# A triangular solve turned round: column updates instead of row sums, its turned copy taken in pieces, some blocks moved from ScalarE to VectorE, and norm factors broadcast by transposes

## The chip, the cores and the metric

The kernel runs on one core of one Trainium2 chip. The metric is the device time of one execution in microseconds; a kernel's time is the median of its runs. Beside those runs stands one execution that was taken with the hardware profiler, and all rows of the trace are from that one.

## The reference

The reference is a small network over 256 tokens of width 1024: a first block of two layers (four gated feed-forward parts, an RWKV-7 time mix in the first layer, a differential attention in the second) and a second block (sliding-window and stick-breaking attention, then a mixture of 16,384 small experts). The change touches two things in it.

The first is the recurrence of the RWKV-7 time mix, per head, with 16 heads of 64 columns:

```python
def step(S, inp):
    r_t, w_t, k_t, v_t, a_t, b_t = inp
    sa = jnp.einsum('bhij,bhj->bhi', S, a_t)
    S = S * w_t[:, :, None, :] + sa[..., None] * b_t[:, :, None, :] + v_t[..., None] * k_t[:, :, None, :]
    return S, jnp.einsum('bhij,bhj->bhi', S, r_t)
```

The kernel does not step through the 256 tokens. It works in chunks of 128 tokens, where the terms `sa` of one chunk solve a triangular system; for that it inverts the 32x32 unit lower-triangular blocks on the diagonal of each head's and chunk's system.

The second is the factor of each RMS norm, `rsqrt(mean(x*x) + eps)`, which is one number per token (or per token and head) and is multiplied onto rows that lie across partitions.

## The kernel before

Activations lie transposed, with 128 of the 1024 columns on the partitions and the 256 tokens along the free axis. Weights come in tiles of 128x1024 (512 KB) by SyncE's queue into three `raw` buffers. Work is written as Python generators that are advanced in turn (`stagger`, `staggered`, `parallel`); this fixes the program order, and the framework's scheduler then lays down one fixed order of instructions for each engine when the kernel is built, with program order as priority. Each engine takes its instructions strictly in that order.

The part around the change, in the time mix (`rwkv`, `keys`, class `Wkv`):

- `rproj` makes the r and the v projections on TensorE. A v projection of one of the eight `d` (two heads each) is 16 matmul instructions (8 tiles, two instructions each in fp32) into one of two PSUM banks `mm`, which ScalarE copies out into `vf` (L526). While v is projected, `prep` for the first two `d` also runs: four transposes (`tr`, L397), their copy, and for each of four systems the matmuls `gr` and VectorE's masked copy `gm` (L1210).
- `chain` runs beside it (`parallel`, 1.25 steps of it for one of `rproj`): first `key(d)` for each `d`, which among other things normalizes k by `gstat_g` and makes `gram`, whose diagonal 32x32 blocks POOL gathers into `bdg`; then `solve`.
- `solve` holds the 128 diagonal blocks (16 heads by 2 chunks by 4 blocks) as one 32x32 matrix on each of the 128 partitions. It turns `bdg` into `sysb` with a 32x32 block transpose, and then for t = 1 to 31 makes row t of the inverse `xs` out of the rows above it: one VectorE multiply of t*t elements (L656), in which `xs` is read with a stride of 32 elements, and one VectorE sum over t (L658). At the end a block transpose writes `xd`; ScalarE copies `xs` with its last two axes swapped into `xr` (L662); a second block transpose writes `xtd` (L663).
- `Wkv.head(d)` then begins, for each `d`, with 16 small copies: the four 32-token blocks of `xd` into `x1`, then those of `xtd` into `xt1` (L1227, ScalarE, tile `xb`, one instruction for four systems of 32x32, eight instructions for each `d`; there are two such pairs of buffers). The first matmuls `lp` read `xt1`; the matmuls `lx` read `x1`. After that come the chains of small matmuls and copies (`ch`, `rt`, `ut`, `sp`), the mean (`mn`), and the norm by `gstat_g`. Up to five heads' generators are in flight.
- `gstat_g` makes a norm's factors: matmuls `smp` with a mask, VectorE's scale (L333), POOL's power -0.5 (L336), for two groups a copy into `re` (L340), and then two fp32 matmuls of 128x128 against the identity, which lay the factors out across the free axis (L345).

Of the kernel before, what the change touches and what calls it, by code (L numbers as in the profile page):

```python
# [6 lines left out]
F32 = mybir.dt.float32  # L7
F32R = mybir.dt.float32r
U32 = mybir.dt.uint32
AF = mybir.ActivationFunctionType  # L10
ALU = mybir.AluOpType
AX = mybir.AxisListType
# [127 lines left out]
def staggered(gens, every, width=99):  # L140
    queue, active, t = list(gens), [], 0
    while queue or active:
        if queue and len(active) < width and (t >= every or not active):
            active.append(queue.pop(0))
            t = 0
        t += 1
        for g in list(active):
            try:
                next(g)
            except StopIteration:  # L150
                active.remove(g)
        yield


def parallel(a, b, ratio):
    debt, live = 0.0, [True, True]
    while any(live):
        if live[0]:
            live[0] = next(a, live) is not live
        debt += ratio if live[0] else 1  # L160
        while live[1] and debt >= 1:
            live[1] = next(b, live) is not live
            debt -= 1
# [10 lines left out]
class Net:  # L174
# [150 lines left out]
    def gstat_g(self, sq, mask, G, scale, eps, op=ALU.add, sb=None):  # L325
        nc = self.nc
        pb = self.smt()
        ps = pb[:, T:T + 2 * G]
        for h in range(2):
            self.mm(ps[:, h * G:(h + 1) * G], sq[:, h * 128:(h + 1) * 128], mask, h == 0, h == 1)  # L330
        yield
        ms = self.small(4)
        nc.vector.tensor_scalar(ms[:, :2 * G], ps, scale, eps, op0=ALU.mult, op1=op)  # L333
        yield
        r = self.small(4)
        nc.gpsimd.tensor_tensor(r[:, :2 * G], ms[:, :2 * G], self.mhalf[:, :2 * G], op=ALU.pow)  # L336
        yield
        if G > 1:
            re = self.tmp("re")
            nc.vector.tensor_copy(re.rearrange("p (a b) -> p a b", a=2 * G),  # L340
                                  r[:, :2 * G, None].to_broadcast([128, 2 * G, 128 // G]))
            yield
        for h in range(2):
            st = re[:, h * 128:(h + 1) * 128] if G > 1 else r[:, h:h + 1].to_broadcast([128, 128])
            self.mm(pb[:, h * 128:(h + 1) * 128], st, self.ident, h == 0, h == 1)  # L345
        yield
        if sb is None:
            return pb[:, :T]
        nc.scalar.activation(sb, pb[:, :T], AF.Copy)
        return sb  # L350
# [232 lines left out]
    def keys(self, er, rproj, aa, cum, ar, bt, kt, xd, xtd, oka, gram):  # L583
        tc, nc, i = self.tc, self.nc, self.i
        vec = self.v
        D = range(8)
        bdg = er.tile([128, 32, 32], F32, name="bdg", tag="sya")
        sysb = er.tile([128, 32, 32], F32, name="sysb")
        pb = er.tile([128, 2, 16], F32, name="pb")
        xs = er.tile([128, 32, 32], F32, name="xsys")  # L590
        flat = lambda a: a.rearrange("p a b -> p (a b)")
        nc.gpsimd.memset(xs, 0.0)
        nc.gpsimd.memset(flat(xs)[:, 0:1024:33], 1.0)
        cmid = cum[:, :, :, 64:65].rearrange("p a b o -> p (a b o)")
        nc.vector.tensor_scalar(pb[:, 0], cmid, E05, None, op0=ALU.mult)
        nc.vector.tensor_scalar(pb[:, 1], cmid, -E05, None, op0=ALU.mult)
        dcy = self.dcy
        v1 = lambda a: a.rearrange("p (c t) -> p c t", c=2)

        ready = set()  # L600

        def key(d):
            kr = kt[:, d].rearrange("p c t -> p (c t)")
            sq = self.tmp("sq")
            nc.scalar.activation(sq, kr, AF.Square, scale=vec("k_k", d))
            yield
            en = self.tmp("en")
            dc = self.small(2)
            nc.scalar.activation(dc[:, 0:1], cum[:, d, 0, 128:129], AF.Exp, scale=-E05, bias=pb[:, 0, 2 * d:2 * d + 1])
            nc.scalar.activation(dc[:, 1:2], cum[:, d, 1, 64:65], AF.Exp, scale=-E05)  # L610
            for c in range(2):
                j = 2 * d + c
                nc.scalar.activation(en[:, c * 128:(c + 1) * 128], cum[:, d, c, 1:], AF.Exp, scale=E05, bias=pb[:, 1, j:j + 1])
                nc.scalar.activation(cum[:, d, c], cum[:, d, c], AF.Exp, scale=-E05, bias=pb[:, 0, j:j + 1])
            ready.add(d)
            rb = yield from self.gstat_g(sq, self.bmask2, 2, 1.0, 1e-24, op=ALU.max)
            nc.vector.tensor_tensor(dcy[:, d:d + 1], dc[:, 0:1], dc[:, 1:2], op=ALU.mult)
            kn = self.tmp("kn")
            nc.vector.scalar_tensor_tensor(kn, kr, vec("k_k", d), rb, op0=ALU.mult, op1=ALU.mult)
            ep = cum[:, d]  # L620
            nc.vector.scalar_tensor_tensor(ar[:, d, :, 0], v1(kn), -1.0, ep[:, :, :128], op0=ALU.mult, op1=ALU.mult)
            t = self.tmp("ka")
            nc.vector.tensor_tensor(t, kn, aa[:, d], op=ALU.mult)
            nc.vector.tensor_tensor(bt[:, d], v1(t), v1(en), op=ALU.mult)
            yield
            ps = []
            for hh in range(2):
                hs = slice(64 * hh, 64 * hh + 64)
                p = self.wkt("bd")
                for c in range(2):  # L630
                    self.mm(p[:, c * 128:(c + 1) * 128], bt[hs, d, c], ar[hs, d, c, 0], c == 0, c == 1)
                ps.append(p)
            t = self.tmp("kb")
            nc.vector.tensor_scalar(t, aa[:, d], vec("k_a", d), oka[:, d:d + 1], op0=ALU.mult, op1=ALU.add)
            nc.vector.tensor_tensor(t, t, kr, op=ALU.mult)
            nc.vector.tensor_tensor(kt[:, d], v1(t), v1(en), op=ALU.mult)
            yield
            for hh in range(2):
                nc.scalar.activation(gram[:, d, 2 * hh:2 * hh + 2], ps[hh][:, :T].rearrange("p (c t) -> p c t", c=2), AF.Copy)
            yield  # L640
            for b in range(4):
                bs = slice(32 * b, 32 * b + 32)
                nc.gpsimd.tensor_copy(bdg[bs, :, 4 * d:4 * d + 4].rearrange("p t h -> p h t"), gram[bs, d, :, bs])
            yield

        def rout(d, p):
            while d not in ready:
                yield
            nc.vector.tensor_tensor(ar[:, d, :, 1], v1(p), cum[:, d, :, 1:], op=ALU.mult)
            yield  # L650

        def solve():
            nc.vector.transpose(flat(sysb), flat(bdg))
            for t in range(1, 32):
                tmp = er.tile([128, 32, 32], F32, name="stmp")
                nc.vector.tensor_tensor(tmp[:, :t, :t], xs[:, :t, :t].rearrange("p j s -> p s j"),  # L656
                                        sysb[:, t, None, :t].to_broadcast([128, t, t]), op=ALU.mult)
                nc.vector.tensor_reduce(xs[:, t, :t], tmp[:, :t, :t], axis=AX.X, op=ALU.add)  # L658
                yield
            nc.vector.transpose(flat(xd), flat(xs))  # L660
            xr = er.tile([128, 32, 32], F32, name="xr", tag="sya")
            nc.scalar.activation(xr, xs.rearrange("p t s -> p s t"), AF.Copy)  # L662
            nc.vector.transpose(flat(xtd), flat(xr))  # L663

        def chain():
            yield from staggered([key(d) for d in D], EVERY["keys"])
            yield from solve()

        parallel(rproj(rout), chain(), EVERY["krat"])
# [485 lines left out]
class Wkv:  # L1155
# [58 lines left out]
    def head(self, d):  # L1214
        net = self.net
        nc, vec = net.nc, net.v
        ar, bt, kt, gg, vf, tab, xd, xtd, gram = self.a
# [3 lines left out]
            yield  # L1221
        pair = self.x1s[d % 2]
        x1, xt1 = pair[:, 0], pair[:, 1]
        for src, dst in ((xd, x1), (xtd, xt1)):
            for b in range(4):
                bs = slice(32 * b, 32 * b + 32)
                nc.scalar.activation(dst[bs, :, bs], src[bs, :, 4 * d:4 * d + 4].rearrange("p t h -> p h t"), AF.Copy)  # L1227
        yield
        while d >= EVERY["nb"] and d - EVERY["nb"] not in self.ended:
            yield  # L1230
# [4 lines left out]
        p = net.wkt("lp")  # L1235
# [6 lines left out]
        p = net.wkt("lx")  # L1242
# [9 lines left out]
        for c in range(2):  # L1252
            bank = net.wkt("ch")
            p, pu, o = (bank[:, 128 * n:128 * n + 128] for n in range(3))
# [45 lines left out]
        p = net.wkt("mn")  # L1300
# [58 lines left out]
```

## Time and profile before

| what | value |
|---|---|
| time, median of 3 runs | 2231.76 us (2227.08 to 2232.41) |
| profiled execution, its own time | 2242.64 us |
| span of the profiled execution | 2240.9 us |
| TensorE matmul busy | 2196.6 us (98%) |
| TensorE weight load busy | 2054.8 us (92%) |
| VectorE busy | 1544.6 us (69%) |
| ScalarE busy | 1121.9 us (50%) |
| GpSimd busy | 77.0 us (3%) |
| mean granted TensorE clock | 0.985 |

The profiled execution took 10.9 us longer than the median run; the span, from its first to its last instruction, is 1.7 us shorter than its own time. Busy times are sums over the span, and a busy TensorE is not one at its peak, since the ends of its matmuls are modelled. The granted clock is a share of full speed: 1.00 is 2.4 GHz and 0.50 is 1.2 GHz.

### The profile page before, as it was taken

Reading aid. Unit: us, or ns where it says so; the run is one execution under the profiler, and the core shown is the slowest. Engines: PE = TensorE matmul, PEld = TensorE weight load, DVE = VectorE, ACT = ScalarE, POOL = GpSimd, SP = SyncE. Lnnn points to the kernel's source line nnn. Section 1 sums busy time; section 2 is a strip of 40 time slices with the busy share of each in tenths; the row PEclk is TensorE's granted clock in tenths of the full one; section 3 lists DMA queues with packets and bytes.
Section 4 is the critical chain, followed back from the end, with each engine's and each line's share of the span. In section 5 each row is a group of like instructions: output and inputs, shape, how many; then the busy total and the mean of one; then the engine's idle time right before and its main releaser. Section 6 shows DMA issues by size and latency. Waiting matters only on the chain.

```text
span 2240.9 us, 40442 instructions
## 1 busy us (share of the span) xinstructions
PE 2196.6 (98%) x16114; PEld 2054.8 (92%) x16114; DVE 1544.6 (69%) x2966; ACT 1121.9 (50%) x2083; POOL 77.0 (3%) x109
## 2 busy tenths in 40 slices
PE   8999999989999999999999999999999999999999
PEld 8998877779999999979999999999999999888887
DVE  6666694666666666476665777899678995666565
ACT  5443723335445444465445664445566664554544
POOL 0000140000000100020000100000000000000000
PEclk9999996999999999999999999999999999999999
DMA  6554321015565455534556345455544445555554
GB/s 212 185 179 135 121 95 38 1 61 192 182 181 182 165 170 176 167 113 160 179 181 194 132 138 184 157 168 178 192 138 139 132 136 185 195 191 197 191 195 150
DMA packets 98588, 351.05 MB, mean 157 GB/s; under 512 B 10944, under 2 KB 12480, under 8 KB 98272
## 3 DMA queue, kind: packets, MB, share of 16 engines
q1 hardware_dynamic: 98400, 348.48, 47.8%
q8 instruction: 126, 2.06, 0.4%
q14 instruction: 62, 0.51, 0.1%
HBM read 347.38 MB, written 1.05 MB: 155 GB/s over the span
## 4 chain that ended last, share of the span: by engine, by line
PE 47%; DVE 5%; issue 1%; ACT 0%; DMA 0%; POOLq 0%; POOL 0%; ACTq 0%
PE mm L243 27%; PE y L243 16%; PE pg L243 3%; DVE wl L258 2%; DVE dm L1125 1%; DVE ex L1130 0%; DVE dm L1128 0%; PE sc L243 0%; PE po L243 0%; DVE v L1093 0%; PE smp L243 0%; PE tr L757 0%; PE psc L243 0%; DVE si L1095 0%; DMA raw<-in_p_u_dram 0%
## 5 line engine op out<-in xcount | busy, mean ns | idle before, releaser
L243 PE MATMUL mm<-xs,wh 128*128 128x256 f32 x6304 | 1159.3, 285 | 13.2 <-ACT wh L255 7.0
L243 PEld LDWEIGHTS mm<-xs,wh 128*128 128x128 f32 x6304 | 986.4, 192 | 20.0 <-ACT wh L255 7.2
L258 DVE TENSOR_TENSOR wl<-raw,wh 128x1024 fp32r<-128x1024 f32 (+1 forms) x633 | 765.3, 1209 | 325.3 <-ACT wh L255 324.1
L255 ACT ACTIVATE wh<-raw 128x1024 fp32r<-128x1024 f32 (+1 forms) x633 | 660.3, 1044 | 594.3 <-PE mm L243 399.5
L243 PE MATMUL mm<-xs,wl 128*128 128x256 f32 x3152 | 894.4, 284 | 2.4 <-DVE wl L258 2.4
L243 PEld LDWEIGHTS mm<-xs,wl 128*128 128x128 f32 x3152 | 605.7, 192 | 3.4 <-DVE wl L258 3.3
L243 PE MATMUL y<-wh,cs 128*128 128x512 f32 x1024 | 273.8, 389 | 0.0
L243 PE MATMUL mm<-hh,wh 128*128 128x256 f32 x1408 | 250.1, 281 | 0.0
L243 PEld LDWEIGHTS y<-wh,cs 128*128 128x128 f32 x1024 | 192.1, 188 | 39.8
L243 PEld LDWEIGHTS mm<-hh,wh 128*128 128x128 f32 x1408 | 215.8, 188 | 0.0
L243 PE MATMUL mm<-hh,wl 128*128 128x256 f32 x704 | 197.8, 281 | 0.0
L243 PE MATMUL y<-wl,cs 128*128 128x512 f32 x512 | 157.5, 389 | 0.0
L243 PEld LDWEIGHTS mm<-hh,wl 128*128 128x128 f32 x704 | 132.5, 188 | 0.0
L243 PE MATMUL mm<-xs,raw 128*128 128x256 f32 x512 | 126.5, 395 | 2.5 <-DVE xs L490 2.5
L243 PEld LDWEIGHTS y<-wl,cs 128*128 128x128 f32 x512 | 96.1, 188 | 20.0
L243 PEld LDWEIGHTS mm<-xs,raw 128*128 128x128 f32 x512 | 96.2, 197 | 17.1 <-DVE xs L490 2.6
L306 ACT ACTIVATE cs<-ga 128x256 fp32r<-128x256 f32 x103 | 43.0, 418 | 136.9 <-PE y L243 136.6
L420 DVE TENSOR_TENSOR gu<-mm,rstd 128x512 f32<-128x512 f32 x88 | 60.8, 691 | 47.0 <-PE mm L243 45.5
L306 ACT ACTIVATE hh<-hv 128x256 fp32r<-128x256 f32 x88 | 36.6, 416 | 104.5 <-DVE hv L425 104.5
L307 DVE TENSOR_TENSOR cs<-ga,cs 128x256 fp32r<-128x256 f32 x103 | 43.7, 425 | 55.1 <-ACT cs L306 55.1
L1040 DVE TENSOR_SCALAR ohb<-iota,xT 128x128 f32<-128x128 f32 x192 | 59.3, 341 | 15.4 <-PE pg L243 13.9
L243 PE MATMUL pg<-ohb,xT 128*128 128x128 f32 x512 | 65.8, 275 | 0.0
(318 smaller groups left out, 1954.0 us busy)
## 6 DMA issues: line engine op xcount, KB each, us to landing
raw<-in_ffn_in_dram SPq DMA_DIRECT2D x176, 512.0 KB, 3.3
raw<-in_p_u_dram SPq DMA_DIRECT2D x128, 512.0 KB, 3.3
raw<-in_p_v_dram SPq DMA_DIRECT2D x128, 512.0 KB, 3.3
raw<-in_ffn_out_dram SPq DMA_DIRECT2D x64, 512.0 KB, 3.6
raw<-in_w_in_dram SPq DMA_DIRECT2D x34, 512.0 KB, 3.3
raw<-in_ffn_out_dram SPq DMA_DIRECT2D x32, 384.0 KB, 3.4
raw<-in_w_rkv_dram SPq DMA_DIRECT2D x24, 512.0 KB, 3.3
raw<-in_w_kv_dram SPq DMA_DIRECT2D x16, 512.0 KB, 3.3
```

What stands on the lines that cost most here:

```text
L243: self.nc.tensor.matmul(out, lhsT, rhs, start=start, stop=stop, skip_group_check=True)
L255: hi = nc.scalar.activation(fh[:rows, :w], raw[:rows, :w], AF.Copy)
L258: lo = nc.vector.tensor_tensor(fl[:rows, :w], raw[:rows, :w], fh[:rows, :w].bitcast(F32), op=ALU.subtract)
L306: nc.scalar.activation(dst[rows, :T], src, AF.Copy)
L307: nc.vector.tensor_tensor(dst[rows, T:], src, dst[rows, :T].bitcast(F32), op=ALU.subtract)
L420: nc.vector.tensor_tensor(t, p.rearrange("p (a b) -> p a b", a=2), box["r"][:, None, :].to_broadcast([128, 2, T]), op=ALU.mult)
L1040: nc.vector.tensor_scalar(b, iota, itp[:, 1, t:t + 1], itp[:, 2, t:t + 1], op0=ALU.is_equal, op1=ALU.mult)
L1125: nc.vector.tensor_tensor(m, iota[:, None, :50].to_broadcast([128, 16, 50]), bf[:, h, :, None].to_broadcast([128, 16, 50]), op=ALU.is_equal)
```

## The change

`solve` goes by columns: at step t, row t of the inverse is final, and its multiples are added to all rows below it. One multiply makes (31-t)*(t+1) products, one add puts them onto those rows; in both the innermost axis has unit stride (or repeats one element). The copy with swapped axes is taken in four pieces, three of them inside the loop, after t = 15, 23 and 28. The block transpose for `xtd` goes ahead of that for `xd`. In `head`, the blocks of `xt1` are copied ahead of those of `x1`, and for d = 0 and 1 VectorE makes the copies instead of ScalarE. In `gstat_g`, the two fp32 matmuls against the identity become two transposes.

```diff
@@ gstat_g
             st = re[:, h * 128:(h + 1) * 128] if G > 1 else r[:, h:h + 1].to_broadcast([128, 128])
-            self.mm(pb[:, h * 128:(h + 1) * 128], st, self.ident, h == 0, h == 1)
+            nc.tensor.transpose(pb[:, h * 128:(h + 1) * 128], st, self.ident)
@@ keys
         def solve():
             nc.vector.transpose(flat(sysb), flat(bdg))
-            for t in range(1, 32):
+            xr = er.tile([128, 32, 32], F32, name="xr", tag="sya")
+            turned = 0
+            for t in range(31):
+                n, w = 31 - t, t + 1
                 tmp = er.tile([128, 32, 32], F32, name="stmp")
-                nc.vector.tensor_tensor(tmp[:, :t, :t], xs[:, :t, :t].rearrange("p j s -> p s j"),
-                                        sysb[:, t, None, :t].to_broadcast([128, t, t]), op=ALU.mult)
-                nc.vector.tensor_reduce(xs[:, t, :t], tmp[:, :t, :t], axis=AX.X, op=ALU.add)
-                yield
+                nc.vector.tensor_tensor(tmp[:, :n, :w], xs[:, t, None, :w].to_broadcast([128, n, w]),
+                                        sysb[:, w:, t, None].to_broadcast([128, n, w]), op=ALU.mult)
+                nc.vector.tensor_tensor(xs[:, w:, :w], xs[:, w:, :w], tmp[:, :n, :w], op=ALU.add)
+                if t in (15, 23, 28):
+                    nc.scalar.activation(xr[:, :, turned:w], xs[:, turned:w].rearrange("p t s -> p s t"), AF.Copy)
+                    turned = w
+                yield
+            nc.scalar.activation(xr[:, :, turned:], xs[:, turned:].rearrange("p t s -> p s t"), AF.Copy)
+            nc.vector.transpose(flat(xtd), flat(xr))
             nc.vector.transpose(flat(xd), flat(xs))
-            xr = er.tile([128, 32, 32], F32, name="xr", tag="sya")
-            nc.scalar.activation(xr, xs.rearrange("p t s -> p s t"), AF.Copy)
-            nc.vector.transpose(flat(xtd), flat(xr))
@@ Wkv.head
-        for src, dst in ((xd, x1), (xtd, xt1)):
+        for src, dst in ((xtd, xt1), (xd, x1)):
             for b in range(4):
                 bs = slice(32 * b, 32 * b + 32)
-                nc.scalar.activation(dst[bs, :, bs], src[bs, :, 4 * d:4 * d + 4].rearrange("p t h -> p h t"), AF.Copy)
+                sv = src[bs, :, 4 * d:4 * d + 4].rearrange("p t h -> p h t")
+                if d < 2:
+                    nc.vector.tensor_copy(dst[bs, :, bs], sv)
+                else:
+                    nc.scalar.activation(dst[bs, :, bs], sv, AF.Copy)
```

## Rows read from the trace of the kernel before

**Rows 1.** The page: its first line.

```profile
span 2240.9 us, 40442 instructions
```

**Rows 2.** Windows: us, busy time (instructions) by engine, PEclk, DMA share, GB/s.

```profile
356.00:397.00 41.00, 41.00 (x186) 32.19 (x186) 10.98 (x28) 16.46 (x39) 0.00 (x0) 0.50 0.00 1
397.00:460.00 63.00, 62.45 (x476) 48.53 (x476) 42.51 (x109) 23.66 (x53) 5.71 (x5) 1.00 0.05 12
```

**Rows 3.** Windows of 2 us around the changes of the granted clock.

```profile
328.00:330.00 2.00, 0.65 (x3) 0.65 (x4) 1.97 (x4) 0.00 (x0) 0.00 (x0) 0.67 0.24 96
...
354.00:356.00 2.00, 0.15 (x1) 0.18 (x2) 0.00 (x0) 1.90 (x5) 0.52 (x1) 1.00 0.27 109
356.00:358.00 2.00, 2.00 (x9) 1.78 (x10) 0.18 (x1) 1.90 (x6) 0.00 (x0) 0.50 0.00 0
...
396.00:398.00 2.00, 2.00 (x15) 1.30 (x14) 0.69 (x2) 0.47 (x2) 0.00 (x0) 0.76 0.00 0
```

**Rows 4.** Waits of TensorE from 296 to 460 us: total, times, longest.

```profile
PE lp L243 <- ACT xb L1227: 4.0, 1, 4.0
PE gr L243 <- DVE gm L1210: 3.1, 2, 2.6
```

**Rows 5.** Timeline of VectorE, the solve: start, us, instruction, [idle before].

```profile
304.13 1.25 DVE L653 STREAM_TRANSPOSE sysb<-bdg 128x1024 f32<-128x1024 f32 x1 [2.54 <-POOL bdg L643]
...
305.61 0.14 DVE L656 TENSOR_TENSOR stmp<-xsys,sysb 128x1 f32<-128x1 f32 x1
305.78 0.15 DVE L658 TENSOR_REDUCE xsys<-stmp 128x1 f32<-128x1 f32 x1
...
328.72 0.57 DVE L1210 COPY_PREDICATED gm<-rtab,gr 128x384 f32<-128x384 uint32 x1
...
345.81 1.81 DVE L656 TENSOR_TENSOR stmp<-xsys,sysb 128x961 f32<-128x961 f32 x1
...
348.01 1.15 DVE L658 TENSOR_REDUCE xsys<-stmp 128x31 f32<-128x961 f32 x1
...
351.28 1.25 DVE L663 STREAM_TRANSPOSE hd<-xr 128x1024 f32<-128x1024 f32 x1 [0.85 <-ACT xr L662]
```

**Rows 6.** Timeline of ScalarE, behind the solve.

```profile
349.24 2.00 ACT L662 ACTIVATE xr<-xsys 128x1024 f32<-128x1024 f32 x1 [7.42 <-DVE xsys L658]
...
351.41 6.93 ACT L1227 ACTIVATE xb<-hd 32x128 f32<-32x128 f32 x16
```

**Rows 7.** Timeline of TensorE: v projections, the first head's begin.

```profile
330.93 5.96 PE L243 MATMUL mm<-xs,raw 128*128 128x256 f32 x16
...
348.10 3.72 PE L243 MATMUL mm<-xs,raw 128*128 128x256 f32 x16
355.85 1.93 PE L243 MATMUL lp<-xb,xs 128*128 128x128 f32 x8 [4.03 <-ACT xb L1227]
```

**Rows 8.** Timeline of TensorE: d=0's mean; d=3's begin and mean.

```profile
395.40 1.06 PE L243 MATMUL mn<-y,base 128*128 128x256 f32 x2
...
405.19 1.11 PE L243 MATMUL lp<-xb,xs 128*128 128x128 f32 x8
...
436.77 0.60 PE L243 MATMUL mn<-y,base 128*128 128x256 f32 x2
```

**Rows 9.** Groups by line and form, 230 to 460 us: busy us, mean ns.

```profile
L635 DVE TENSOR_TENSOR kb<-kb,kt 128x256 f32<-128x256 f32 x8 | 3.3, 415 | 0.1
```

**Rows 10.** Tile `smp`: VectorE's instruction in each norm; ns min/median/max.

```profile
L333 DVE TENSOR_SCALAR sm<-smp x33: 143/155/163, 17.7 to 1400.8; 128x4 f32<-128x4 f32 x25, 128x2 f32<-128x2 f32 x8
```

**Rows 11.** Timeline of TensorE: one norm's broadcast, and `prep`'s four transposes.

```profile
314.28 0.38 PE L397 MATMUL tr<-base,vf 128*128 128x128 f32 x2
...
314.72 3.62 PE L243 MATMUL mm<-xs,raw 128*128 128x256 f32 x16
...
1236.95 0.61 PE L243 MATMUL smp<-base,re 128*128 128x128 f32 x4
1237.40 0.51 PE L243 MATMUL smp<-base,sq 128*128 128x2 f32 x4
```

## The prediction

> **What bounds the kernel now.** I read the windows first: over the span TensorE is the engine that is nearly always busy, so a stretch is worth something only where TensorE waits or runs at its lower clock. One place has both. The profiled execution takes 2242.64 us around a span of 2240.9 [rows 1], and its granted clock averages 0.985; from 356 to 397 us it is 0.50, the 1.2 GHz level, and in those 41 us TensorE gets through 186 instructions, 4.5 per us, where the 63 us behind them, at 2.4 GHz, hold 476, 7.6 per us [rows 2]. Narrower windows show what it did before: the clock is still full at 354 to 356, where TensorE does almost nothing, and half from 356 on; it comes back inside 396 to 398. It falls once before that, inside 328 to 330, again in a stretch with little work [rows 3].
>
> The waits of TensorE name the two pauses: 4.0 us for ScalarE's blocks of the first head, and 3.1 us, 2.6 of it at once, for VectorE's masked copy `gm` [rows 4]. Both come from the solve. VectorE's timeline shows it from 304.13 to 352.5 us, with `gm` stuck between its steps [rows 5]. Behind it ScalarE takes 2.00 us to turn the result and then 0.43 us for each of the first 16 blocks (6.93 / 16) [rows 6]. The v projections, TensorE's cover for all this, end at 351.82; `lp` begins at 355.85 [rows 7].
>
> **The solve.** Fixed cost and slope come from its own rows [rows 5]. The sum of 1 element takes 0.15 us and that of 961 takes 1.15, so 1.04 ns per element; a two-operand instruction with unit strides fits this line (256 elements: 0.15 + 0.27 = 0.42, measured 415 ns [rows 9]). The strided multiply goes from 0.14 at 1 element to 1.81 at 961: 1.74 ns per element. Dependent instructions start 0.03 us after the one before ends.
> Old: the squares from 1 to 31 add up to 10,416 elements, so 10,416 x (1.74 + 1.04) ns = 29.0 us, plus 62 instructions x 0.18 = 11.2, together 40; the rows give 43.5 from 305.61 to 349.16, with `gm` and the r products in between. New: the steps hold 5,456 elements twice, 62 instructions again: 2 x 5,456 x 1.04 ns = 11.3, plus 11.2, so 22.5 us, about 25 with guests. Bounds: if short rows ran at the strided price, 2 x 5,456 x 1.74 = 19 + 11.2 = 30 us, 33 with guests. The solve ends near 331, at the latest 339, instead of 349.
>
> The copy in parts: (2.00 - 0.15) / 1,024 = 1.8 ns per element. The pieces hold 512, 256, 160 and 96 elements: 1.1, 0.6, 0.4 and 0.3 us. Only the last lies behind the solve, the rest beside it. What they add is a wait: ScalarE is in order, and a piece that waits for its step holds up whatever stands behind it, the copies of v out of the two `mm` banks. One projection is 3.72 us [rows 7], and a second bank lets TensorE go on that long.
>
> Then a block transpose of 1.25 us for `xtd`, the second for `xd` behind it. The first four blocks for `xt1` on VectorE: no row has this copy there; bounds are the unit-stride line (0.15 + 128 x 1.04 ns = 0.28) and the strided one (0.15 + 128 x 1.74 = 0.37). I take 0.37, since it reads with the stride. So `lp` could begin at 331 + 0.3 + 2 x 1.25 + 4 x 0.37 = 335, and at the late bound at 343. All 16 blocks cost VectorE 16 x 0.37 = 6 us, ScalarE is rid of 6.9. Both are hidden: the v projections last longer. Without that cover, if these began at 351, they would cost what the old ones did. No transfer is added, and no queue of SyncE is passed.
>
> **First term: the changeover, 8 us (4.0 to 9.4).** With blocks ready before 343, `lp` begins when the v projections end: 4.03 us gone. The projections themselves end earlier: the waits for `gm` (3.1) should shrink, since no step of the solve is longer than 0.15 + 256 x 1.04 ns = 0.42 us now, and with them the fall of the clock at 328, which cost at least 5.96 - 3.72 = 2.2 us [rows 7]. Of these 5.3 us I take 4, as `gm`'s place in VectorE's order is fixed by the build; the bounds are none and all.
>
> **Second term: the clock behind it, 11 us (8 to 16).** Without the pause the heads should start at 2.4 GHz. TensorE at the fast rate would do the 186 instructions in 186 / 7.6 = 24.6 us instead of 41: 16.4 less [rows 2]. But at first few heads are in flight, and a head is a chain of small steps. The first head took 395.40 - 355.85 = 39.6 us from `lp` to its mean, the fourth, at full clock, 436.77 - 405.19 = 31.6 [rows 8]: 8.0 less. I take 11, nearer to the chain's value, for the first heads are chains. Nothing behind this stage waits for anything but TensorE, so what is won here stays.
>
> **Third term: the broadcasts, 7 us (0 to 8).** There are 33 norms of this kind, one VectorE instruction each [rows 10]. In a dense stretch the four fp32 instructions move TensorE on by 1237.40 - 1236.95 = 0.45 us; `prep`'s four transposes take 314.72 - 314.28 = 0.44, so 0.22 for two [rows 11]. 33 x 0.23 = 7.6 us; I take 7, as a few stand in pauses where TensorE waits anyway. The lower bound, nothing, would be if all did.
> Of the clock, the trace has transposes at 314 us with a full clock and no fall behind them [rows 11]. The Trainium skill says, in "TensorE: Matmul & The Clock Gate", Part 4: PE-mode transpose, that transposes do not count as TensorE activity for the clock the way matmuls do. The rows neither show nor exclude this: the transposes there are short and lie among matmuls. By that rule, two transposes less to count in a thin stretch could bring a fall forward; it is a rival below.
>
> **The sum.** 8 + 11 + 7 = 26 us: 2242.64 - 26 = 2216.6 for a profiled execution. The median of the runs is 10.9 below the profiled time, so 2231.76 - 26 = 2205.8, say 2206. Its own range, with every bound: 2231.76 - 33 to 2231.76 - 12, so 2198 to 2220.
>
> **Rivals.**
> *The clock falls all the same (0.17).* At the changeover TensorE still meets a pause, since `lp`, the masked copy into `zt`, `lx` and their copies follow one another, with two heads at most to fill the gaps. For it: pauses of 2.6 and 4.0 us were enough [rows 3, 4]. Against it: from 397 on the same kind of work kept the full clock for 63 us [rows 2]. Then the second term is gone and half of the first: 4 + 7 = 11, so 2221.
> *The order puts `lp` too early: slower (0.07).* The build knows the shorter solve, and may put the first head's `lp` ahead of the last three v projections. TensorE is in order, so it would wait there for the solve, with projections behind it. If it is late by w, TensorE stands for w, the clock falls, and three projections at half clock cost 3 x 2.2 = 6.7 us; the heads stay at half clock. Against this stand the old pause, 4, and the third term, 7: 2231.8 + w + 6.7 - 11. It is slower by over 0.3% (about what a measurement of this kernel can tell from no change) from w = 11 us on, as at w = 12: 2239.5. For it: the build had `gm` between two steps of the solve while TensorE waited 2.6 us for it [rows 4, 5]. Against: v has the earlier place in program order.
> *The changeover does not move (0.07).* ScalarE's pieces or VectorE's 16 blocks stand behind something late, and `lp` begins as before; only the broadcasts gain, or not even those: 2225 to 2232.
> *Transposes do not hold the clock (0.04).* One more fall, at the price of one at 328, 2.2 us or a little more: 2209. This is the case in which the Trainium skill's rule above would matter.
> *Heads begin under the v projections (0.07).* If the order lets `lp` at 335 fill TensorE's gaps, the first chains overlap with up to 347 - 335 = 12 us of projections: up to 2194.
>
> **How the numbers follow.** The forecast has 0.58. The range of 2195 to 2226 holds it, the fallen clock, the transposes' fall, a part of the early heads and the near edge of the unmoved changeover. 0.3% is 6.7 us, so faster ends at 2225: the forecast, the fallen clock, the clock rule and the early heads, 0.86 together, of which I take 0.05 off for terms that come out small together: 0.81. Slower is 0.08, the rest 0.11 the same.
>
> **What would show it.** VectorE's solve from 305 to about 331, its last multiply near 0.2 us instead of 1.81; three pieces of `xr` inside it; TensorE's wait for `xb` gone and `lp` at 346 to 349; a clock of 1.00 where 356 to 397 had 0.50; `smp` from `re` with half the instructions. It is wrong if the clock is half again behind the v projections, if ScalarE's copies of v wait behind a piece of `xr`, or if the new rows cost more than 1.74 ns per element.

## The result, and the profile after

The changed kernel takes 2212.07 us (2211.21 to 2214.31, 4 runs) beside 2232.09 us (2227.08 to 2235.92, 4 runs) for the kernel before: 20.0 us less, ratio 0.9917, 95% interval 0.9896 to 0.9938. Forecast were 2206.0 us and a range of 2195 to 2226. The profiled execution after takes 2211.49 us at a mean granted clock of 0.994. Executions of the kernel before differ among themselves in that clock, from 0.982 (2251 us) to 0.994 (2226 us), and this has to be kept in mind for every difference below.

The page of the kernel after, its first line [rows 1]:

```profile
span 2209.7 us, 40311 instructions
```

The windows of the kernel after, from the first `lp` on, beside [rows 2] (us, busy time and instructions of TensorE, weight load, VectorE, ScalarE and GpSimd, granted clock, DMA share, GB/s):

```profile
348.00:370.00 22.00, 22.00 (x182) 17.65 (x182) 10.40 (x27) 13.53 (x32) 0.00 (x0) 1.00 0.08 25
370.00:397.00 27.00, 27.00 (x201) 20.36 (x200) 17.74 (x49) 12.79 (x31) 2.18 (x2) 1.00 0.00 1
397.00:460.00 63.00, 57.61 (x451) 45.07 (x451) 39.86 (x106) 16.44 (x36) 6.35 (x6) 1.00 0.11 35
```

The clock is 1.00 where it was 0.50. The first 22 us hold 182 instructions; the kernel before needed 41 us for 186.

TensorE's waits after, 296 to 460 us, the largest two [rows 4]:

```profile
PE smp L345 <- DVE re L340: 2.6, 2, 1.8
PE tr L397 <- ACT vf L526: 2.3, 1, 2.3
```

Neither the wait for `xb` nor that for `gm` is there. A new one inside the v projections is: `tr` waits 2.3 us for a copy of v. The timelines tell why. VectorE after, the solve and what follows [rows 5] (start, us, instruction, [idle before]):

```profile
307.03 0.21 DVE L659 TENSOR_TENSOR stmp<-xsys,sysb 128x31 f32<-128x31 f32 x1
...
319.45 0.42 DVE L659 TENSOR_TENSOR stmp<-xsys,sysb 128x256 f32<-128x256 f32 x1
...
332.40 0.19 DVE L661 TENSOR_TENSOR xsys<-xsys,stmp 128x31 f32<-128x31 f32 x1
332.62 1.25 DVE L668 STREAM_TRANSPOSE hd<-xsys 128x1024 f32<-128x1024 f32 x1
333.79 1.20 DVE L667 STREAM_TRANSPOSE hd<-xr 128x1024 f32<-128x1024 f32 x1
334.92 2.86 DVE L1234 COPY xb<-hd 32x128 f32<-32x128 f32 x5
```

ScalarE after, beside the solve [rows 6]:

```profile
319.51 1.09 ACT L663 ACTIVATE xr<-xsys 128x512 f32<-128x512 f32 x1 [3.67 <-DVE xsys L661]
320.50 0.38 ACT L526 ACTIVATE vf<-mm 128x256 f32<-128x256 f32 x1
...
326.53 0.66 ACT L663 ACTIVATE xr<-xsys 128x256 f32<-128x256 f32 x1 [1.93 <-DVE xsys L661]
...
330.41 0.49 ACT L663 ACTIVATE xr<-xsys 128x160 f32<-128x160 f32 x1 [1.31 <-DVE xsys L661]
...
332.62 0.31 ACT L666 ACTIVATE xr<-xsys 128x96 f32<-128x96 f32 x1 [1.73 <-DVE xsys L661]
```

TensorE after, the same stretch up to the first head [rows 7] and its mean [rows 8]:

```profile
314.99 3.62 PE L243 MATMUL mm<-xs,raw 128*128 128x256 f32 x16
320.93 0.44 PE L397 MATMUL tr<-base,vf 128*128 128x128 f32 x2 [2.32 <-ACT vf L526]
...
344.71 3.72 PE L243 MATMUL mm<-xs,raw 128*128 128x256 f32 x16
348.26 0.94 PE L243 MATMUL lp<-xb,xs 128*128 128x128 f32 x7
...
370.27 0.67 PE L243 MATMUL mn<-y,base 128*128 128x256 f32 x2
```

The projection of v ended at 318.61, but ScalarE stood 3.67 us at the first piece of `xr`, with the copy of v behind it (320.50), and `tr` needs that copy. The last projection ends at 348.4 (344.71 + 3.72) instead of 351.82, and `lp` starts at once. The solve took 332.59 - 307.03 = 25.6 us.

Where the time went, by stages: key 8 is POOL's power in the last key's norm, head 1 and head 8 the same in the heads' norms, kv the eight norms of a later stage. The profiled execution of before was a long one (2242.64), so the table also has a second execution of it (2234.28, described under "The clock by itself"), and two kernels of the experiments.

| stage, us | before | before, second | solve only | all but broadcasts | after |
|---|---|---|---|---|---|
| start to key 8 | 293.8 | 294.3 | 295.0 | 295.1 | 296.7 |
| key 8 to first `lp` | 62.1 | 62.1 | 57.4 | 54.9 | 51.6 |
| `lp` to head 8 | 131.4 | 121.3 | 113.5 | 113.2 | 110.3 |
| kv 1 to kv 8 | 64.6 | 64.6 | 64.6 | 64.6 | 63.2 |
| span | 2240.9 | 2232.6 | 2222.2 | 2217.1 | 2209.7 |

The changeover and the heads behind it hold nearly all of it; kv shows the broadcasts alone, (64.6 - 63.2) / 7 = 0.2 us for each norm. And the stretch behind `lp` differs by 10 us between two executions of the same kernel before.

In one row the kernel after is slower: it comes to key 8 2.9 us later. Its clock fell ahead of the solve, in a window where the profile of before kept it (before, then after):

```profile
240.00:260.00 20.00, 19.67 (x116) 15.79 (x114) 12.57 (x27) 13.50 (x25) 0.00 (x0) 1.00 0.43 142
240.00:260.00 20.00, 19.68 (x93) 15.60 (x92) 10.00 (x20) 11.94 (x22) 0.00 (x0) 0.83 0.39 132
```

Seven kernels of the experiments show a fall there too (0.83 to 0.87 from 250 to 260 us), three of them with the old solve, while two with the new solve do not. It seems to belong to the execution and not to the change, and it enters differences between the spans in the table.

### The profile page after: what moved, and what is told of

It is laid out like the page before. It is cut to its first block, busy times and chain, and to the rows that moved or that the text cites. A ratio compares the mean times of both kernels' runs of the same rounds, so it can differ in the third digit from the quotient of the medians.

```text
span 2209.7 us, 40311 instructions
## 1 busy us (share of the span) xinstructions
PE 2169.1 (98%) x16048; PEld 2032.6 (92%) x16048; DVE 1533.2 (69%) x2982; ACT 1116.3 (51%) x2070; POOL 78.0 (4%) x109
## 3 DMA queue, kind: packets, MB, share of 16 engines
q1 hardware_dynamic: 98400, 348.48, 49.2%
## 4 chain that ended last, share of the span: by engine, by line
PE 48%; DVE 5%; issue 1%; ACT 0%; DMA 0%; POOLq 0%; POOL 0%; ACTq 0%
PE mm L243 28%; PE y L243 16%; PE pg L243 3%; DVE wl L258 2%; DVE dm L1130 1%; DVE ex L1135 0%; PE sc L243 0%; DVE dm L1133 0%; PE po L243 0%; DVE v L1098 0%; PE tr L762 0%; PE psc L243 0%; DMA raw<-in_p_u_dram 0%; DVE si L1100 0%; PE smp L243 0%
```

## The experiments

**Each part alone.** The norms' transposes put into the kernel before:

```diff
-            self.mm(pb[:, h * 128:(h + 1) * 128], st, self.ident, h == 0, h == 1)
+            nc.tensor.transpose(pb[:, h * 128:(h + 1) * 128], st, self.ident)
```

> The kernel before with nothing but the norm factors broadcast by transposes. Theory A (TensorE's time is what counts in nearly every place where a norm is made; 33 norms by 0.23 us): 7 us faster, 2225. Theory B (the broadcasts stand in latency chains or beside waits, so TensorE's saved time is hidden): 2 us or less, 2230 to 2232. Both expect the half clock behind the v projections to stay, with about 4 us of waiting for the first blocks.

Measured: 2232.81 us (2222.83 to 2248.37, 12 runs) beside 2230.23 (2226.26 to 2251.22, 35 runs), ratio 0.9999 (0.9966 to 1.0031): nothing to be seen. But the clock differs. The runs' mean clock is 0.987 in the median, before's is 0.992; nine of the twelve are at 0.987 or less, and seven of the thirty-five of before. At equal clock, 0.987, its four runs take 2231.65 to 2233.43, and the six runs of before at that clock, beside this and later experiments, took 2237.07 to 2240.09: 6.2 us more in the means (2238.4 and 2232.3). In its profile the stretch behind the pause is at half clock:

```profile
354.00:386.00 32.00, 30.79 (x138) 24.51 (x138) 8.27 (x20) 14.05 (x34) 0.14 (x1) 0.52 0.00 1
```

So at equal clock the gain is there, and a lower clock hides it. Do the transposes bring that clock about? The norms' transposes nearest to this stretch are those of the last key and of the first head:

```profile
297.64 0.44 PE L345 MATMUL smp<-base,re 128*128 128x128 f32 x2
...
401.61 0.44 PE L345 MATMUL smp<-base,re 128*128 128x128 f32 x2
```

Between 298 and 401 us there is none, so none stands in the stretch at half clock. TensorE's pause ahead of `lp` was 4.8 us in this profile and 4.0 in that of before. The question is taken up once more at the end.

The reverse, the kernel after with the fp32 matmuls back in the norms (the same two lines exchanged):

> The changed kernel with the two fp32 matmuls back in the norm. Theory A: 7 of the 20 us are lost again, 2219, and the clock behind the v projections stays at 1.00. Theory B: 2 us or less lost, 2212 to 2214.

Measured: 2218.51 us (12 runs), ratio 0.9936 (0.9915 to 0.9957), which is theory A. Against after's 2212.07 the broadcasts are worth 6.4 us; against the two kernels below that come nearest to after (2213.6, 2214.1), 4.5 to 4.9.

The column solve alone in the kernel before, with one turned copy at its end, old blocks and old norms (the cut shows how its loop differs from the changed one):

```diff
             for t in range(31):
...
                 nc.vector.tensor_tensor(xs[:, w:, :w], xs[:, w:, :w], tmp[:, :n, :w], op=ALU.add)
-                if t in (15, 23, 28):
-                    nc.scalar.activation(xr[:, :, turned:w], xs[:, turned:w].rearrange("p t s -> p s t"), AF.Copy)
-                    turned = w
                 yield
```

> The kernel before with the solve by columns alone: one turned copy at the end, blocks of all heads by ScalarE, old order of the blocks, old broadcasts. Theory A (the solve ends near 333 us, 18 us before TensorE needs it, so pieces and VectorE's blocks are hidden and worth nothing): the wait for the first blocks is gone, the clock stays at 1.00 behind it, and the time is that of the changed kernel without its broadcasts, 2219 or 13 us faster. Theory B (pieces, order and VectorE's blocks carry a part): a wait for the blocks of 1 us or more stays, and the gain is 8 us or less, 2224 or more.

Measured: 2219.93 us (12 runs), ratio 0.9946 (0.9923 to 0.9968), so 10.3 us of the change are the solve in the medians. As theory A had it, the wait for the first blocks is gone; one of 2.4 us for `gm` stays. Pieces and blocks add 1.4 (2219.93 to 2218.51), within what these runs can tell apart.

**Pieces and blocks, one taken out of the kernel after at a time.** No early piece (the three lines above removed), then the blocks on ScalarE (`if False:` for `if d < 2:`), then no first piece (`if t in (23, 28):`):

> The changed kernel with the turned copy in one instruction at the end of the solve, as before, instead of in four pieces. Theory A (the early pieces cost a wait: TensorE stood 2.3 us for a copy of v that ScalarE held behind the first piece; the 1.7 us longer last copy is hidden under the v projections): 1 to 2.3 us faster than the changed kernel, 2210 to 2211, with that wait gone. Theory B (the pieces shorten the path to the first head): 1 to 2 us slower than it, 2213 to 2214.

> The changed kernel with the first two heads' blocks made by ScalarE again, in the new order. Theory A (hidden: VectorE had them ready at 342 us and TensorE came at 348): the same time, 2211 to 2213, no wait for blocks, clock 1.00. Theory B (ScalarE, which also copies v, is late with them): a wait for blocks of 1 to 4 us comes back, and with it the half clock, 2216 to 2222.

> The changed kernel with three pieces instead of four: the first (after t = 15) is joined to the second (after t = 23). Theory A: the copy of v is no longer held behind a piece, TensorE's wait of 2.3 us is gone, 2210 to 2211. Theory B (that wait is made up for later, since the first head is not waiting for TensorE alone): no difference, 2212.

Measured, side by side: 2216.43 us (8 runs; ratio 0.9915, 0.9882 to 0.9948), 2214.06 (6; 0.9896, 0.9856 to 0.9936) and 2213.61 (6; 0.9894, 0.9854 to 0.9935). The first goes the way of theory B and further than it said; the second lies between its two theories, without a wait for blocks; the third is nearer to theory B. The blocks on VectorE are worth nothing that shows, and neither is the first piece. All pieces together are worth 2.4 to 2.8 us beside these two kernels and 4.4 beside after; pieces and blocks together showed only 1.4 above. The wait only changes its place. TensorE's waits without the first piece, 296 to 460 us:

```profile
PE gr L243 <- DVE gm L1215: 2.0, 1, 2.0
```

And TensorE's timeline without any early piece:

```profile
338.97 0.79 PE L243 MATMUL gr<-ar,bt 64*128 64x128 f32 x2 [2.96 <-DVE gm L1212]
...
341.82 5.56 PE L243 MATMUL mm<-xs,raw 128*128 128x256 f32 x16
...
351.72 1.05 PE L243 MATMUL lp<-xb,xs 128*128 128x128 f32 x8
```

With the first piece, TensorE waits for a copy of v behind ScalarE's piece (2.3 us, also with the blocks on ScalarE); without it, for the masked copy behind VectorE's transposes and blocks; without any, 3.0 us for that copy, with a projection at half clock behind (5.56 us), and `lp` 3.5 us later. Taking out both the first piece and VectorE's blocks should then leave no wait:

> The changed kernel with three pieces of the turned copy (after t = 23 and 28, and the rest) and all blocks by ScalarE. Theory A (the two waits that are left inside the v projections are a copy of v behind the first piece, and masked copies behind the first heads' blocks on VectorE; both are gone here): 2 us faster than the changed kernel, 2210 to 2211, and no wait over 1 us inside the v projections. Theory B (ScalarE's blocks now hold up copies of v): the wait moves once more, 2212 to 2215.

Measured: 2212.47 us (2208.53 to 2219.87, 6 runs; ratio 0.9928, 0.9912 to 0.9944), no better than after in the median: theory A's wait went, and theory B's time came. The largest wait that is left before the heads, 296 to 362 us:

```profile
PE bd L243 <- DVE bt L624: 0.7, 2, 0.6
```

The wait inside the v projections did go, and `lp` begins earliest of all (49.2 us behind key 8). Its windows behind that:

```profile
350.00:360.00 10.00, 10.00 (x81) 7.60 (x81) 5.12 (x14) 6.74 (x16) 0.00 (x0) 1.00 0.01 2
360.00:370.00 10.00, 10.00 (x44) 7.89 (x46) 2.60 (x7) 2.01 (x6) 0.00 (x0) 0.51 0.00 1
370.00:380.00 10.00, 10.00 (x68) 7.51 (x68) 4.18 (x13) 3.73 (x9) 0.98 (x1) 0.64 0.01 2
```

The clock fell at 360, with no wait of TensorE above 0.6 us since 296: a fall can come inside the heads' small steps without a recorded pause. Three of its runs, at clock 0.995 to 0.996, took 2208.5 to 2210.4, three at 0.991 took 2214.6 to 2219.9.

The blocks' new order and engine alone in the kernel before:

```diff
-        for src, dst in ((xd, x1), (xtd, xt1)):
+        for src, dst in ((xtd, xt1), (xd, x1)):
...
+                if d < 2:
+                    nc.vector.tensor_copy(dst[bs, :, bs], sv)
...
```

> The kernel before with only the first heads' blocks by VectorE and the turned ones first; the old solve ends at 352.5 us as before. The first head's first matmuls should begin 1.5 to 2.5 us earlier. Theory A (a pause of about 2 us remains, and what decides is whether the clock falls in it): 2 us faster if it falls (2230), 8 to 12 us if it does not (2220 to 2224). Theory B (the clock is worth nothing here): 2 us faster in either case.

Measured: 2230.93 us (12 runs), ratio 0.9988 (0.9960 to 1.0017): nothing, and key 8 to `lp` is 61.6 instead of 62.1, so the 1.5 to 2.5 us did not come. TensorE's wait ahead of `lp` is 1.9 instead of 4.0, but its waits for `gm` are 4.1 instead of 3.1: here too a wait moved.

**The clock by itself.** The kernel before, with work added that is thrown away: eight unread fp32 matmuls on copied v ahead of the first `lp`, meant to fill TensorE's pause.

```diff
+        if d == 0:
+            pd = net.wkt("dm")
+            for q in range(8):
+                net.mm(pd[:, :T], net.ident, vf[:, 7], q == 0, q == 7)
         p = net.wkt("lp")
```

> The kernel before, with eight matmuls of 256 columns whose result nobody reads (16 instructions, 3.7 us) put in front of the first head's first matmuls, where TensorE waits 4 us. Nothing is taken away: solve, blocks and broadcasts are the old ones, and the first head begins no earlier. Theory A (the half clock behind the pause is itself worth 8 us or more): the clock is 1.00 behind the pause and the time falls by 5 to 11 us, to 2221 to 2227. Theory B (the first heads are chains that do not notice the clock): 0 to 1 us, 2231 to 2233, also where the clock is full.

Measured: 2233.29 us (12 runs), ratio 1.0002 (0.9981 to 1.0023). It did not test what it was meant to. Its timeline of TensorE:

```profile
363.26 6.07 PE L243 MATMUL dm<-vf,base 128*128 128x256 f32 x16 [6.14 <-ACT vf L526]
369.17 1.05 PE L243 MATMUL lp<-xb,xs 128*128 128x128 f32 x8
```

The last copy of v stands behind 16 blocks on ScalarE, so the filler waited 6.14 us itself and `lp` came 13 us later than before. That the time stayed the same is still telling: `lp` to head 8 took 110.8 us. With the seventh projection's v (`vf[:, 6]`), which is copied earlier, the rest as before:

> As the run that filled the pause, but the eight unread matmuls take an earlier copy of v, so that they can begin at 351.8 us, when the v projections end, instead of waiting for the last copy of v, which stands behind 16 blocks on ScalarE. The first head begins no earlier than before, at about 356 us. Theory A (the half clock behind the pause is the price): the clock is 1.00 from 356 us on, the stretch from the first head's first matmuls to the last head's norm takes 113 us as it did with old broadcasts at full clock, instead of 124 to 131, and the time falls by 8 to 13 us, to 2218 to 2224. Theory B (worth nothing by itself): 2230 to 2233.

Measured: 2225.71 us (2224.05 to 2232.19, 11 runs) beside 2229.25 (17 runs), ratio 0.9990 (0.9981 to 0.9999). `lp` stands at 355.46, not earlier than before, and the first window of [rows 2] now reads:

```profile
356.00:397.00 41.00, 40.15 (x310) 31.38 (x309) 22.17 (x58) 22.55 (x53) 2.35 (x2) 1.00 0.01 2
```

Now 310 instructions at full clock instead of 186 at half; `lp` to head 8 takes 114.2 us. Against the profiled execution of before that is 17 us, yet the median gains only 3.5, and by the ratio 2.2 (0.2 to 4.2): less than theory A, more than theory B. The kernel before once more, one execution:

> The kernel before once more, unchanged, for a second profile of it. Theory A (how long the clock stays at half behind the pause differs from execution to execution, and the first profile had a long one): a half-clock stretch shorter than 41 us and a time nearer 2230 than 2242. Theory B (the half stretch is fixed and the 10 us lie elsewhere): 41 us again.

It took 2234.28 us, as theory A expected, and its windows show why:

```profile
356.00:364.00 8.00, 7.58 (x34) 6.97 (x34) 1.59 (x3) 6.72 (x17) 0.00 (x0) 0.57 0.00 0
364.00:374.00 10.00, 10.00 (x80) 7.48 (x79) 5.20 (x14) 5.26 (x12) 0.00 (x0) 1.00 0.01 2
374.00:377.00 3.00, 3.00 (x18) 2.45 (x18) 0.35 (x1) 0.28 (x1) 0.00 (x0) 0.50 0.00 0
377.00:397.00 20.00, 20.00 (x156) 15.34 (x155) 11.64 (x31) 8.53 (x20) 1.18 (x1) 0.99 0.01 2
```

The same pause (4.07 us here), but behind it half clock for some 8 and then 3 us, not 41.

**Do the transposes lower the clock?** The filled pause and the transposes together, in the kernel before (the two edits above):

> The kernel before with two edits: the 8 unread matmuls on the copied seventh v projection ahead of the first head's lp (work that is added and thrown away), and the transposes in the norms. Alone, the first measured 2225.7 us and the second 2232.8. Theory: the transposes save about 6 us wherever the clock holds, and alone they showed nothing in the median because the stretch behind the pause ran at half clock. Then both together should give 2225.7 - 6 = 2219 to 2221 us, with a granted clock of 1.00 from the start of lp to 430 us and 63.2 us from the first to the last kv norm. Rival: the transposes themselves lower the clock. Then it falls behind the v projections here too, with nothing else to cause it, and the time is 2225 us or more.

Measured: 2222.04 us (2219.18 to 2240.05, 12 runs), ratio 0.9960 (0.9935 to 0.9985); nine of the runs lie between 2219.2 and 2222.5. Against the filled pause alone that is 3.7 us in the medians, 6.7 by the two ratios (0.9990 and 0.9960, each to the kernel before beside it) and 6.3 in the spans (2223.6 to 2217.3), with kv at 63.2. The same window:

```profile
356.00:397.00 41.00, 40.14 (x315) 31.41 (x316) 22.22 (x59) 23.69 (x56) 2.19 (x2) 1.00 0.01 2
```

In this profile the clock holds through the heads with the transposes in place, and their gain comes out. In two of the twelve runs, 2235.0 and 2240.1 us, the mean clock was 0.987 and 0.984; neither of these was profiled, so where it fell is not known. Among the 17 runs of before beside them six were at such a clock. That the transposes lower the clock is not shown. Why it was lower in most runs when they stood alone in the kernel before stays open.

## Why the prediction was right, and where it was off

**Direction and mechanism: right.** The column solve took 25.6 us (25 with guests expected), its last step 0.19 us, its longest multiply 0.42 (two adds took 0.82 and 0.71, see the last section); the strided bound, 33, did not come. The pieces took 1.09, 0.66, 0.49 and 0.31 us (1.1, 0.6, 0.4, 0.3). The v projections ended at 348.4, `lp` began at 348.26 (346 to 349; ends are modelled), and the clock was 1.00 behind it. One of the prediction's own signs of being wrong did come: a copy of v stood behind a piece of `xr`. The prediction had covered this by the second `mm` bank, but TensorE did not wait for a bank. It waited for the copied v itself, which `tr` reads.

**First term, 8 us: measured 7.2 with the old broadcasts** (key 8 to `lp`, 62.1 to 54.9), 10.5 between the profiled executions of before and after. Counted from the start of the span, `lp` comes 5.9 us earlier without the broadcasts and 7.6 in the kernel after (355.85 to 348.26), for both of these profiles have the fall ahead of the solve. The pause went whole; of the waits in front of it a part came back as the wait of 2.3 us behind ScalarE's piece. "Hidden" was right for VectorE's blocks: they are worth nothing either way.

**Second term, 11 us: wrong in size. It is 2 to 6 on the median.** The mechanism is shown: with the pause filled and `lp` no earlier, the heads ran at full clock. The price was read from one profiled execution, whose 41 us at half clock are a long case. There the head stretch did lose 131.4 - 113.2 = 18 us, beyond even the upper bound of 16; the second execution lost 8; filling the pause gave 3.5 in the medians (2.2 by the ratio), and the change without broadcasts 11.7 (2230.23 to 2218.51), of which 7.2 or 5.9 are the first term, so 4.5 or 5.8. The step that failed is the one from "2242.64 - 26 = 2216.6 for a profiled execution" to "2231.76 - 26 = 2205.8". The profiled execution exceeded the median by 10.9 us, and the term was read from its long half-clock stretch, so it held that excess. The second execution bears this out: its span is 8.3 us shorter, and the stretch behind `lp` alone is 10.1 shorter. The excess should have been taken from the term before it went onto the median. Against the profiled execution the sum was too small: 2216.6 was forecast, 2211.49 came. The other reading within it was off the other way: the first head's chain, priced by the fourth head at 31.6 us, took 22.0 at full clock (370.27 - 348.26), probably because fewer heads shared TensorE with it; no run tests that.

**Third term, 7 us: 4.5 to 6.4 by leaving it out of the kernel after,** 0.2 us for each norm in kv, where 0.23 was worked out. Put into the kernel with the filled pause it gave 3.7 in the medians.

**Sum.** 7.2 + 4.5 + 6.4 = 18 beside the 20.0 measured and the 26 forecast. This does not test the terms: 4.5 is what was left over, so the three must add up to 2230.23 - 2212.07. It shows where the miss lies: nearly all of it in the second term.

**The rivals.** The clock's fall for all that (2221) did not come in the profile of after, though the kernel with three pieces shows that it can. `lp` was not put too early, nor did heads run under the projections. The rival that transposes do not hold the clock had one more fall in it; the profiles of after and of the last experiment kept 1.00 through the heads, with transposes in all their norms, and the falls behind the v projections in two other profiles, of the transposes alone and of the three pieces, came where no norm's transpose had run for over 50 us. The Trainium skill states in "TensorE: Matmul & The Clock Gate", Part 4: PE-mode transpose, that transposes do not count as activity for the clock the way matmuls do. No run here tests that rule, since these transposes lie among matmuls.

## What to carry to other kernels

A fall of the clock behind a pause has no fixed price: before the time of one profiled execution goes into a sum, see how it stands to the median, and take the excess out of the term that holds it. When a wait of an in-order engine is removed, list what the next instruction on each engine waits for, since here three layouts of the same copies each left a wait of 2 to 3 us, in one of two places. A part that shows nothing alone may be covered by another: compare runs at equal granted clock, or put it in once the cover is gone.

## What the runs showed of the hardware

Some VectorE instructions took far longer while GpSimd worked. VectorE in the kernel after, neighbours of nearly the same size in the solve, then two parts of the block copies:

```profile
314.25 0.40 DVE L659 TENSOR_TENSOR stmp<-xsys,sysb 128x231 f32<-128x231 f32 x1
314.68 0.82 DVE L661 TENSOR_TENSOR xsys<-xsys,stmp 128x231 f32<-128x231 f32 x1
...
316.42 0.42 DVE L659 TENSOR_TENSOR stmp<-xsys,sysb 128x247 f32<-128x247 f32 x1
...
317.79 0.71 DVE L661 TENSOR_TENSOR xsys<-xsys,stmp 128x252 f32<-128x252 f32 x1
...
335.08 1.46 DVE L1234 COPY xb<-hd 32x128 f32<-32x128 f32 x1
...
339.33 3.04 DVE L1234 COPY xb<-hd 32x128 f32<-32x128 f32 x10
```

GpSimd in the kernel after, its work beside the first five of them:

```profile
314.64 0.61 POOL L1179 COPY zt<-base 128x512 f32<-128x512 f32 x1
...
316.07 1.38 POOL L1178 MEMSET gm<- 128x1536 f32 x1
317.40 0.82 POOL L1179 COPY zt<-base 128x512 f32<-128x512 f32 x1
...
335.05 1.42 POOL L1178 MEMSET gm<- 128x1536 f32 x1 [15.94 <-DVE hd L667]
```

One block copy took 1.46 us, as long as GpSimd's memset beside it, where the ten at 339.33, with GpSimd idle, took 0.30 each. It takes half of the 2.86 us of the five at 334.92. The adds at 314.68 and 317.79 took 0.82 and 0.71 beside a GpSimd copy, where the multiplies just ahead of them, of the same sizes, took 0.40 and 0.42. But the multiply at 316.42 ran beside a memset at its usual 0.42, so not every overlap costs. The cause was not tested.

The kernel with the late filler shows the clock while TensorE stands still. Its windows of 2 us:

```profile
358.00:360.00 2.00, 0.00 (x0) 0.00 (x0) 0.59 (x1) 1.89 (x6) 0.97 (x2) 1.00 0.53 209
360.00:362.00 2.00, 0.00 (x0) 0.00 (x0) 0.00 (x0) 1.90 (x6) 0.00 (x0) 0.81 0.00 0
362.00:364.00 2.00, 0.74 (x2) 0.65 (x3) 0.00 (x0) 1.16 (x3) 0.00 (x0) 0.50 0.00 0
...
368.00:370.00 2.00, 2.00 (x14) 1.81 (x13) 0.00 (x0) 0.00 (x0) 0.00 (x0) 0.99 0.00 0
```

The clock fell while TensorE stood, and was back within the 16 dense instructions behind the pause (6.07 us), whereas the heads' thin chains behind a shorter pause stayed at half clock for up to 41 us.
